# Attention's normalisation moved to a compact reciprocal by way of DRAM, and the SSD decay difference moved to a bias

## The chip, the cores and the metric

The kernel runs on one NeuronCore of a Trainium2 chip. The engines are named as in the profile: PE (TensorE, with its weight loads PEld), DVE (VectorE), ACT (ScalarE), POOL (GpSimd), and SP (SyncE), which issues all DMAs. Times are device microseconds of one launch. Of the kernel before there are three timed runs.

## The reference

Two layers of a hybrid block over 1024 tokens and 256 context tokens, width 1024, in fp32. Each layer makes all branches with one projection, runs an SSD scan in both directions, attention with 12 query heads on 4 key heads, and a convolution branch, and projects the joined result back.

```python
def attend(q, keys, vals):                      # per block of queries
    s = jnp.einsum('bqkrd,bskd->bkrqs', qi, keys) * scale
    p = jax.nn.softmax(s, axis=-1)
    return jnp.einsum('bkrqs,bskd->bqkrd', p, vals)
...
attn_lat = attend(ql, [kl, kc], [vl, vc]) * jax.nn.silu(ga)     # 1024 queries, 1280 keys
attn_ctx = attend(qc, kc, vc) * jax.nn.silu(ga_c)               # first layer only: 256 queries, 256 keys
...
# SSD, in chunks of 128 tokens
cum  = jnp.cumsum(dt * A, axis=2)
seg  = cum[:, :, :, None] - cum[:, :, None, :]
lmat = jnp.exp(jnp.where(mask, seg, -jnp.inf))
y_diag = jnp.einsum('bclsg,bclsgr,bcsgrp->bclgrp', cb, lmat, xdt)
```

The change touches the division in the softmax, which is made after the product with the values, and `seg`.

## The kernel before

Each layer has four stages: the norm and the input projection (`phase_b`), in which the convolutions run on VectorE beside the matmuls; attention (`attn`) together with the SSD scan (`ssd`); and the output projection (`out_half`) in two halves of 512 columns. Intermediate tensors go through DRAM (`q_d`, `k_d`, `ga_d`, `ya_d`, `cum_d` and others).

The instructions are not in program order. Each piece of code sets a due time with `at(us)`, and a scheduler places the instructions of each engine by that time and by its own estimate of when they are ready. The order is fixed at build: an engine, SP's queue too, runs its list in order, and an instruction that waits holds all behind it.

Attention is cut into units: a pair of heads `p` (six) and a block `g` of 256 queries. The first layer has five blocks a pair, four of latent tokens with ten key tiles and one of context tokens with two; the second layer has four. That makes 30 + 24 = 54 units. Four generators interleave. `maxima` takes the row maxima of unit i+2: score matmuls `q_a` by `k_a` into PSUM tiles `m` (four banks), emptied by VectorE into `a_sm`. `scores` makes the scores of unit i again, transposed, ScalarE puts their exponentials into `a_p`, and VectorE or GpSimd add the tiles up in `a_ac`; `a_a2` (in the profile `a_a`) is the sum of the two halves of that. `values` multiplies `a_p` by the values `vs` into half of a PSUM tile `t` (two buffers) and loads the gate `a_g`. `finish`, one unit later, sums `a_a` over the keys with a matmul by a matrix of twos into the other half of `t`. That gives twice the denominator, which the 64 partitions of a head all hold, since `ga_d` holds twice the silu. VectorE inverts it (`a_rc`), multiplies, GpSimd multiplies by the gate, and SP stores to `ya_d`.

In `ssd`, per chunk, four blocks of six heads are loaded from `cum_d` spread over the partitions (`s_cb`, two buffers); GpSimd subtracts the cumulative sum of the partition's own token, ScalarE takes Relu and Exp in place (`s_e`), and GpSimd multiplies by the masked product `s_cm`. PE uses `s_e` in the matmuls `x<-s_e,s_xd`. Ten chunks with output in the first layer, eight in the second. All matmuls of `q_a`, `k_a` and the weights are in fp32r; `a_p` by `vs`, `a_a` by `twos` and `s_e` by `s_xd` are fp32, and each of those stands as two instructions in the trace.

Of the kernel before, what the change touches and what calls it, by code (L numbers as in the profile page):

```python
# [10 lines left out]
AF = mybir.ActivationFunctionType  # L11
ALU = mybir.AluOpType
# [14 lines left out]
AHEAD = 2  # L27
FLAG = 7
NG = [0, 1]
A2B = 1  # L30
GATP = True
GB = 2
XLAG = 34
PVB = (4, 6)
DM = 1024
# [125 lines left out]
def build(tc, a, out, depth=DEPTH, dump=None):  # L161
    nc = tc.nc
    es = ExitStack()
    V, S, G, P, Y = nc.vector, nc.scalar, nc.gpsimd, nc.tensor, nc.sync
# [9 lines left out]
    def mk(p, shape, tag, dt=F32, bufs=None):  # L174
        uid[0] += 1
        k = {} if bufs is None else {"bufs": bufs}
        return p.tile(shape, dt, tag=tag, name=f"{tag}_{uid[0]}", **k)
# [8 lines left out]
    def dr(shape, name, dt=F32):  # L186
        t = dp.tile(shape, dt, tag=name, name=name)
        if dump is not None:
            dump[name] = t
        return t  # L190

    def mm(o, l, r, start, stop):
        P.matmul(o, l, r, start=start, stop=stop)  # L193
# [4 lines left out]
    def act(o, i, f, **k):  # L198
        S.activation(o, i, f, **k)  # L199
# [28 lines left out]
    twos = mk(cp, [128, 64], "twos")  # L228
# [35 lines left out]
    ys_d = dr([6, 128, T], "ys_d")  # L264
    ya_d = dr([6, 128, T], "ya_d")
    yc_d = dr([4, 128, T], "yc_d")
    gt_d = [dr([2, DM], f"gt_d{l}") for l in range(depth)]

    def rs_pow(o, i, scale, tmp, n):
# [440 lines left out]
    def ssd(l, sp, c0, sv):  # L710
# [3 lines left out]
        dt, cum, ec, et, wd = sv  # L714
# [11 lines left out]
        def bc(x, n=NH, w=HD):  # L726
            return x.unsqueeze(2).to_broadcast([128, n, w])
# [27 lines left out]
        for c in [8, 9] + list(range(8)):  # L755
# [3 lines left out]
            if c < 8 or not last:  # L759
# [7 lines left out]
                ps = mk(px, [128, 512], "x")  # L767
# [12 lines left out]
                for g in range(2):  # L780
                    for d in range(2):
                        h0 = 12 * d + 6 * g
                        cb = mk(sp, [128, 6, 128], "s_cb", bufs=2)
                        src = cum_d[24 * c + h0:24 * c + h0 + 6, :].rearrange("h t -> (h t)")
                        Y.dma_start(out=cb.rearrange("p h t -> p (h t)"),
                                    in_=src.unsqueeze(0).to_broadcast([128, 768]))
                        e = mk(sp, [128, 6, 128], "s_e", bufs=4)
                        G.tensor_tensor(e, cb, bc(cum[:, c, h0:h0 + 6], 6, 128), ALU.subtract)
                        act(e, e, AF.Relu, scale=-1.0)
                        act(e, e, AF.Exp, scale=-1.0)  # L790
                        G.tensor_tensor(e, e, cm[:, d, g].unsqueeze(1).to_broadcast([128, 6, 128]), ALU.mult)
                        E[d, g] = e
                yo = mk(sp, [128, 768], "s_yo", bufs=1)
                G.tensor_tensor(hv(yo), hv(xt), bc(rc(l, "d")), ALU.mult)
                for d, hin in enumerate((hf, hb[c])):
# [3 lines left out]
                    for g in range(2):  # L799
                        ps = mk(px, [128, 512], "x")  # L800
                        mm(ps[:, 0:384], cT[:, g, :], hin[:, 384 * g:384 * g + 384], True, True)
                        h0 = 12 * d + 6 * g
# [5 lines left out]
                for g in range(2):  # L808
                    ps = mk(px, [128, 512], "x")
                    for f3 in range(3):  # L810
                        f = 3 * g + f3
# [17 lines left out]
                ps = mk(px, [128, 512], "x")  # L829
# [74 lines left out]
    def attn(l, ap, c0, pre):  # L904
# [3 lines left out]
        def key_tiles(i):  # L908
            return range(NT) if units[i][1] < 4 else range(8, NT)

        def kv(i, x):
            return (2 * units[i][0] + x) // 3
# [31 lines left out]
        pts, acs = {}, {}  # L944


        def scores(i):
            qa, qb = qst.pop(i)
            pts[i] = {}
            kt = key_tiles(i)  # L950
            ng = NG[i % len(NG)] if len(kt) > 2 else 0
            ac = [mk(ap, [128, 2, 512], f"a_ac{x}") for x in range(2)] if len(kt) > 2 else None
            prev = []
            same = kv(i, 0) == kv(i, 1)
            for b in kt:
                ps = mk(pm, [128, 512], "m")
                for x in range(1 if same else 2):
                    ka, kb = kst[kv(i, x)]
                    o = ps if same else ps[:, 256 * x:256 * x + 256]
                    ra = qa.rearrange("p x t q -> p (x t q)") if same else qa[:, x].rearrange("p t q -> p (t q)")  # L960
                    rb = qb.rearrange("p x t q -> p (x t q)") if same else qb[:, x].rearrange("p t q -> p (t q)")
                    mm(o, ka[:, b, :], ra, True, False)
                    mm(o, kb[:, b, :], rb, False, True)
                if b % 2 == 0:
                    pt2 = mk(ap, [128, 2, 512], "a_p", bufs=PTB)
                act(pt2[:, b % 2], ps, AF.Exp)
                pts[i][b] = pt2[:, b % 2]
                if b % 2:
                    j = b // 2
                    if not prev or j == ng + 1:  # L970
                        prev.append(pt2)
                    else:
                        e, o = (G, ac[0]) if j <= ng else (V, ac[1])
                        e.tensor_tensor(o, prev[-1], pt2, ALU.add)  # L974
                        prev[-1] = o
                yield
            if len(prev) > 1:
                V.tensor_tensor(ac[1], prev[0], prev[1], ALU.add)  # L978
                prev = [ac[1]]
            a2 = mk(ap, [128, 512], "a_a2", bufs=A2B)  # L980
            V.tensor_tensor(a2, prev[0][:, 0], prev[0][:, 1], ALU.add)
            acs[i] = a2
            yield

        def values(i):
            p, g = units[i]
            kt = key_tiles(i)
            gat = mk(ap, [128, 256], "a_g", bufs=GB)
            Y.dma_start(out=gat, in_=ga_d[p][:, 256 * g:256 * g + 256])
# [13 lines left out]
        def finish(i, ps, gat):  # L1003
            p, g = units[i]
            a2 = acs.pop(i)
            for y in range(2):
                mm(ps[64 * y:64 * y + 64, 1, :], twos[:, 0:64], a2[:, 256 * y:256 * y + 256], True, True)
            rc_ = mk(ap, [128, 256], "a_rc", bufs=1)
            V.reciprocal(rc_, ps[:, 1])  # L1009
            V.tensor_tensor(rc_, ps[:, 0], rc_, ALU.mult)  # L1010
            (G if GATP else V).tensor_tensor(gat, gat, rc_, ALU.mult)
            Y.dma_start(out=ya_d[p][:, 256 * g:256 * g + 256], in_=gat)

        t0 = c0
# [18 lines left out]
        for i in range(nu):  # L1033
            at(t0)
            prep(i + AHEAD + 1, t0 - 4)
            w = (13.2 if units[i][1] < 4 else 3.4) * AT_PACE
            ga = maxima(i + AHEAD) if i + AHEAD < nu else ()
            gb = scores(i)
            vq.append(values(i))
            nb = len(key_tiles(i))  # L1040
            na = 0 if i + AHEAD >= nu else 13 if units[i + AHEAD][1] < 4 else 5
            ia = 0
            for s in range(nb):
                at(t0 + w * s / nb)
                next(gb)
                while ia < na and ia * (nb - 1) <= s * na:
                    next(ga)
                    ia += 1
                step += 1
                if step > VLAG:  # L1050
                    pump()
                if fin and s == FLAG % nb:
                    finish(*fin.pop(0))
            for _ in gb:
                pass
            for _ in ga:
                pass
            t0 += w
        while vq:
            pump()  # L1060
        while fin:
            finish(*fin.pop(0))
# [58 lines left out]
    def layer(l, nh, b0):  # L1121
# [8 lines left out]
        ap = pool(st, f"ap{l}")  # L1130
        sp = sr.enter_context(tc.tile_pool(name=f"sp{l}", bufs=1, side="right"))
        ssd(l, sp, c0, sv)
        sr.close()
        yp = sr.enter_context(tc.tile_pool(name=f"yp{l}", bufs=1, side="right"))
# [72 lines left out]
```

## Time and profile before

| what | value |
|---|---|
| three runs | 2912.45, 2925.26, 2928.9 us |
| median | 2925.26 us |
| the profiled execution's own time | 2925.86 us |
| its span | 2924.0 us |
| mean granted TensorE clock | 0.976 |
| first attention stage, from the span's start | 826 to 1385 us |
| second attention stage | 2240 to 2745 us |

The page's first part gives the busy time of each engine, the second part the same in 40 equal slices (a digit is tenths of the slice; PEclk is the granted clock). In a row of groups the columns are line, engine, operation, output and input tile, shape and count, then busy time in us and mean ns of one, then the idle time before them and who ended it. A matmul's length overlaps with its neighbours'. In a row of waits the three numbers are the total us, the times, and the longest. In a row of windows each engine's busy time stands with its count of instructions; behind them the granted clock, the DMA share and GB/s.

### The profile page before, as it was taken

To read this page: it belongs to the slowest core of one execution; us is meant where nothing else is said; L and a number is where in the kernel's file an instruction comes from. 1 tells how busy PE (TensorE), PEld (TensorE's weight loads), DVE (VectorE), ACT (ScalarE), POOL (GpSimd) and SP (SyncE) were. 2 spreads that over 40 slices of the span, in tenths; PEclk is the share of its full clock that TensorE was granted. 3 is DMA by queue.
4 is the path that set the end of the run, shared out by engine and by line. 5 is a ranking of instruction groups with operands and counts; after the bars stand their busy time and mean duration, and the time that the engine had idled before them with its cause. 6 is when DMAs were issued, how large, how long until landed. Compare 5 with 4: busy or idle time off the path is not lost. (4 is left out here: it accounts for less than half of the span.)

```text
span 2924.0 us, 41060 instructions
## 1 busy us (share of the span) xinstructions
PE 2775.7 (95%) x15708; PEld 2058.5 (70%) x15708; DVE 2167.2 (74%) x2987; ACT 1068.0 (37%) x1801; POOL 1167.3 (40%) x832
## 2 busy tenths in 40 slices
PE   5999998999999999899999999999998999999998
PEld 3888876888855555565787998877886565555676
DVE  4576899973288889887545577999834889898744
ACT  4212221222245555454335322222223455644532
POOL 2244122232166767662112353122322676775111
PEclk8999998999999999999999999999999999999999
DMA  6541111223342323223745322113335232321654
GB/s 237 191 160 66 56 55 62 92 92 112 101 144 84 102 68 104 67 76 99 213 153 161 122 77 68 56 55 98 111 118 168 74 98 77 95 64 43 185 154 144
DMA packets 284035, 314.44 MB, mean 108 GB/s; under 512 B 27606, under 2 KB 219190, under 8 KB 282814
## 3 DMA queue, kind: packets, MB, share of 16 engines
q1 hardware_dynamic: 283838, 311.82, 33.5%
q8 instruction: 123, 2.02, 0.3%
q14 instruction: 74, 0.61, 0.1%
HBM read 236.25 MB, written 75.50 MB: 107 GB/s over the span
## 5 line engine op out<-in xcount | busy, mean ns | idle before, releaser
L193 PE MATMUL m<-hh,wth 128*128 128x512 f32 (+1 forms) x1440 | 534.9, 371 | 0.1
L193 PE MATMUL m<-hl,wth 128*128 128x512 f32 (+1 forms) x1440 | 533.4, 370 | 0.0
L193 PE MATMUL m<-hh,wtl 128*128 128x512 f32 (+1 forms) x1440 | 532.7, 370 | 0.0
L199 ACT ACTIVATE a_p<-m 128x512 f32<-128x512 f32 x492 | 289.0, 595 | 374.0 <-PE m L193 370.6
L208 DVE SCALAR_TENSOR_TENSOR cac<-up,cmw,cac 128x1295 f32<-128x1295 f32 (+1 forms) x240 | 385.4, 1627 | 2.0
L935 DVE TENSOR_REDUCE a_sm<-m 128x1 f32<-128x512 f32 (+1 forms) x600 | 332.5, 582 | 46.9 <-PE m L193 45.0
L359 POOL TENSOR_TENSOR wtl<-wr,wth 128x1024 fp32r<-128x1024 f32 x68 | 200.3, 2945 | 406.6 <-ACT wth L199 406.6
L193 PE MATMUL t<-a_p,vs 128*64 128x256 f32 x1968 | 324.0, 405 | 0.7 <-DVE a_rc L1010 0.3
L193 PEld LDWEIGHTS m<-hh,wth 128*128 128x128 f32 x1440 | 274.0, 190 | 48.0 <-ACT th L199 0.5
L193 PEld LDWEIGHTS m<-hh,wtl 128*128 128x128 f32 x1440 | 273.5, 190 | 48.3
L193 PEld LDWEIGHTS m<-hl,wth 128*128 128x128 f32 x1440 | 273.8, 190 | 47.4
L193 PE MATMUL m<-q_a,k_a 128*128 128x512 f32 (+1 forms) x656 | 259.7, 406 | 6.1 <-DVE a_sm L935 4.6
L193 PE MATMUL m<-k_a,q_a 128*128 128x512 f32 (+1 forms) x600 | 247.0, 437 | 13.6 <-DVE a_sm L935 9.8
L193 PE MATMUL m<-woh,yh 128*128 128x512 f32 x576 | 225.8, 395 | 8.2 <-issue 3.3
L193 PE MATMUL m<-woh,yl 128*128 128x512 f32 x576 | 228.8, 398 | 4.4 <-DVE yl L1099 4.3
L193 PE MATMUL m<-wol,yh 128*128 128x512 f32 x576 | 226.5, 394 | 0.0
L193 PE MATMUL m<-q_b,k_b 65*128 65x512 f32 (+1 forms) x656 | 218.8, 344 | 0.0
L193 PEld LDWEIGHTS m<-q_a,k_a 128*128 128x128 f32 x656 | 125.9, 192 | 107.1 <-issue 52.0
L193 PEld LDWEIGHTS t<-a_p,vs 128*64 128x64 f32 x1968 | 104.3, 136 | 133.9 <-issue 95.3
L193 PEld LDWEIGHTS m<-k_a,q_a 128*128 128x128 f32 x600 | 113.5, 195 | 113.3 <-issue 45.2
L199 ACT ACTIVATE wth<-wr 128x1024 fp32r<-128x1024 f32 (+1 forms) x84 | 89.3, 1064 | 256.3 <-DMA wr<-in_wfm 134.5
L193 PE MATMUL m<-wth,hh 128*128 128x256 f32 (+1 forms) x608 | 173.7, 288 | 0.6 <-DVE c_qn L474 0.5
(239 smaller groups left out, 5604.4 us busy)
## 6 DMA issues: line engine op xcount, KB each, us to landing
wr<-in_wfm SPq DMA_DIRECT2D x68, 512.0 KB, 3.6
s_cb<-cum_d SPq DMA_DIRECT2D x72, 384.0 KB, 3.7
ada_w<-in_adaw SPq DMA_DIRECT2D x32, 512.0 KB, 4.2
wor<-in_wout SPq DMA_DIRECT2D x64, 256.0 KB, 3.1
s_x<-xt_d SPq DMA_DIRECT2D x38, 384.0 KB, 3.0
yf<-ys_d SPq DMA_DIRECT2D x36, 384.0 KB, 4.0
yf<-ya_d SPq DMA_DIRECT2D x36, 384.0 KB, 4.2
yf<-yc_d SPq DMA_DIRECT2D x36, 256.0 KB, 2.9
```

The costliest lines, as they stand in the source:

```text
L193: P.matmul(o, l, r, start=start, stop=stop)
L199: S.activation(o, i, f, **k)
L208: V.scalar_tensor_tensor(o, i, s, i1, op0, op1)
L359: (e or G).tensor_tensor(lo[:, s], raw, hi[:, s].bitcast(F32), ALU.subtract)
L935: V.tensor_reduce(sm[:, 2 * x + t, j:j + 1], ps[:, 0:kn], axis=AX.X, op=ALU.max)
```

## The change

In `finish`, the two halves of the last sum are no longer added on VectorE: PE multiplies both by `twos` and adds them in PSUM. ScalarE copies the whole of `t` (the product with the values and the denominators) to SBUF, `a_un`, with a single buffer. One row of denominators per head is stored to DRAM (`dn_d`), loaded again as 32 partitions of 16 (`a_r`), inverted there by VectorE, stored to `rn_d`, and loaded spread over 64 partitions per head (`a_rb`). GpSimd multiplies the gate first by the copy, then by the inverse. The gate tile gets a third buffer. The sum of a context unit is now its tile `a_p` itself, and that of a full unit `a_ac`, which keeps its single buffer.

In `ssd`, the subtraction on GpSimd is gone. ScalarE takes Relu directly from `s_cb`, head by head, with the cumulative sum as bias: six instructions of 128 columns where one of 768 stood.

```diff
-A2B = 1
-GATP = True
-GB = 2
+GB = 3
...
+    dn_d = [dr([2, 256], f"dn_d{i}") for i in range(30)]
+    rn_d = [dr([2, 256], f"rn_d{i}") for i in range(30)]
...
                         e = mk(sp, [128, 6, 128], "s_e", bufs=4)
-                        G.tensor_tensor(e, cb, bc(cum[:, c, h0:h0 + 6], 6, 128), ALU.subtract)
-                        act(e, e, AF.Relu, scale=-1.0)
+                        for j in range(6):
+                            act(e[:, j], cb[:, j], AF.Relu, scale=-1.0, bias=cum[:, c, h0 + j:h0 + j + 1])
                         act(e, e, AF.Exp, scale=-1.0)
...
-            a2 = mk(ap, [128, 512], "a_a2", bufs=A2B)
-            V.tensor_tensor(a2, prev[0][:, 0], prev[0][:, 1], ALU.add)
-            acs[i] = a2
+            acs[i] = prev[0]
...
             a2 = acs.pop(i)
+            for k in range(2):
+                for y in range(2):
+                    mm(ps[64 * y:64 * y + 64, 1, :], twos[:, 0:64], a2[:, k, 256 * y:256 * y + 256], k == 0, k == 1)
+            un = mk(ap, [128, 2, 256], "a_un", bufs=1)
+            act(un, ps, AF.Copy)
             for y in range(2):
-                mm(ps[64 * y:64 * y + 64, 1, :], twos[:, 0:64], a2[:, 256 * y:256 * y + 256], True, True)
-            rc_ = mk(ap, [128, 256], "a_rc", bufs=1)
-            V.reciprocal(rc_, ps[:, 1])
-            V.tensor_tensor(rc_, ps[:, 0], rc_, ALU.mult)
-            (G if GATP else V).tensor_tensor(gat, gat, rc_, ALU.mult)
+                Y.dma_start(out=dn_d[i][y:y + 1, :], in_=un[64 * y:64 * y + 1, 1, :])
+            G.tensor_tensor(gat, gat, un[:, 0], ALU.mult)
+            r = mk(ap, [32, 16], "a_r", bufs=2)
+            Y.dma_start(out=r, in_=dn_d[i].rearrange("y (a q) -> (y a) q", q=16))
+            V.reciprocal(r, r)
+            Y.dma_start(out=rn_d[i].rearrange("y (a q) -> (y a) q", q=16), in_=r)
+            rb = mk(ap, [128, 256], "a_rb", bufs=1)
+            for y in range(2):
+                Y.dma_start(out=rb[64 * y:64 * y + 64], in_=rn_d[i][y:y + 1, :].to_broadcast([64, 256]))
+            G.tensor_tensor(gat, gat, rb, ALU.mult)
             Y.dma_start(out=ya_d[p][:, 256 * g:256 * g + 256], in_=gat)
```

The scheduler makes a new order for the two attention stages from this; ahead of the first one, TensorE's order is the same. Three places follow, in the order of the built programs. A count behind a row is equal instructions in a row, and an fp32 matmul counts once here.

TensorE in the second layer, where the ones-matmul of a unit stands between the scores and values of the next. Before:

```order
L193 MATMUL m_22126<-q_a_21588,k_a_20937 128x512
L193 MATMUL m_22126<-q_b_21589,k_b_20938 128x512
L193 MATMUL t_21932<-a_a_4309_22062,twos_80 64x256 x2
L193 MATMUL t_22092<-a_p_22103,vs_19305 64x256 x2
L193 MATMUL m_22131<-k_a_20937,q_a_21912 128x256
L193 MATMUL m_22134<-q_a_21588,k_a_20937 128x512
```

After, one such place:

```order
L194 MATMUL v_22235<-idr_76,q_g_22232 128x128 x4
L191 MATMUL t_22089<-a_ac_4184_22074,twos_80 64x256 x4
L191 MATMUL m_22287<-k_a_19797,q_a_22069 128x512
L191 MATMUL t_22260<-a_p_22275,vs_19795 64x256
L191 MATMUL m_22290<-k_a_19797,q_a_22069 128x512
```

Four matmuls by `twos` stand where two stood, and read `a_ac` itself.

ScalarE in the first layer, where the fifth pair's context unit (`a_p_11100` before, `a_p_12235` after) follows its last full unit and the sixth pair begins. Before:

```order
L199 ACTIVATE a_p_11100<-m_11110 128x512
L199 ACTIVATE s_e_7873<-s_e_7873 128x768 x2
L199 ACTIVATE q_a_11093<-v_11088 128x512
L199 ACTIVATE q_b_11094<-v_11088 64x512
L199 ACTIVATE q_g_11331<-q_t_11329 128x4x64
L199 ACTIVATE s_of_7820<-s_yz_7779 128x768
L199 ACTIVATE s_e_7880<-s_e_7880 128x768 x2
L199 ACTIVATE s_e_7887<-s_e_7887 128x768 x2
L199 ACTIVATE a_p_11188<-m_11183 128x512
```

After:

```order
L197 ACTIVATE a_p_12235<-m_12245 128x512
L197 ACTIVATE q_a_12226<-v_12221 128x512
L197 ACTIVATE q_b_12227<-v_12221 64x512
L197 ACTIVATE q_g_12466<-q_t_12464 128x4x64
L197 ACTIVATE a_un_12299<-t_12075 128x512
L197 ACTIVATE a_un_12417<-t_12244 128x512
L197 ACTIVATE a_p_12332<-m_12329 128x512
L197 ACTIVATE a_p_12332<-m_12342 128x512
```

The copies of the full unit and of the context unit stand one behind the other, in one buffer, ahead of the next unit's first exponential. The same pair stands at each of the first five context units.

SP's queue in the second layer. Before, the store of a unit's result and the loads around it:

```order
L785 DMA s_cb_19985<-cum_d 128x768
L785 DMA s_cb_19992<-cum_d 128x768
L873 DMA q_t_22543<-q_d_125 128x2x128
L828 DMA ys_d<-s_yo_19814 128x6x128
L1012 DMA ya_d<-a_g_21768 128x256
L989 DMA a_g_22090<-ga_d_137 128x256
L720 DMA s_b_19967<-bt_d 128x256
```

After:

```order
L1010 DMA dn_d_155<-a_un_22847 1x256 x2
L764 DMA s_cT_20655<-cT_d 128x2x128
L1013 DMA a_r_22852<-dn_d_155 32x16
L1015 DMA rn_d_185<-a_r_22852 32x16
L1018 DMA a_rb_22856<-rn_d_185 64x256 x2
L785 DMA s_cb_20545<-cum_d 128x768
L1020 DMA ya_d<-a_g_22600 128x256
L785 DMA s_cb_20556<-cum_d 128x768
L987 DMA a_g_23124<-ga_d_137 128x256
```

The six transfers of a unit's denominators stand in the queue, each but the first waiting for the one before it to land, and the decay loads `s_cb` stand behind them.

## The prediction

> **What bounds the kernel now.** I read the page's busy line and its slices first, to see which engine is full and where.
>
> ```profile
> PE 2775.7 (95%) x15708; PEld 2058.5 (70%) x15708; DVE 2167.2 (74%) x2987; ACT 1068.0 (37%) x1801; POOL 1167.3 (40%) x832
> ...
> PE   5999998999999999899999999999998999999998
> ...
> DVE  4576899973288889887545577999834889898744
> ```
>
> TensorE is full nearly throughout. The change lies in the two attention stages (slices 12 to 19 and 31 to 38), so the view of windows comes next, cut to them.
>
> ```profile
> core 0: us, PE busy (x) PEld busy (x) DVE busy (x) ACT busy (x) POOL busy (x), PEclk, DMA share, GB/s
> 826.00:1385.00 559.00, 531.35 (x3313) 312.57 (x3314) 479.57 (x673) 284.73 (x483) 352.03 (x212) 0.97 0.28 85
> 2240.00:2745.00 505.00, 494.10 (x3032) 286.82 (x3031) 449.10 (x634) 262.80 (x449) 322.01 (x188) 0.99 0.29 90
> ```
>
> Of 1064 us TensorE is idle for 27.65 + 10.90 = 38.55. VectorE is busy 87%, ScalarE 51%, GpSimd 63%. So a gain can only come out of TensorE's idle time and its lowered clock (0.97 and 0.99), and each matmul added is paid almost whole. The waits of TensorE say who makes it idle:
>
> ```profile
> PE m L193 <- DVE a_sm L935: 14.4, 18, 2.2
> ...
> PE t L193 <- DVE a_a L981: 13.0, 9, 3.6
> ```
>
> Both are VectorE: the row maxima that empty score banks (`a_sm`), and the halves' sum (`a_a`) that the ones-matmul waits for. One boundary after a short context unit, in the timeline, shows how the second arises:
>
> ```profile
> 917.33 1.74 DVE L1009 RECIPROCAL a_rc<-t 128x256 f32<-128x256 f32 x1
> ...
> 918.99 0.91 DVE L981 TENSOR_TENSOR a_a<-a_p 128x512 f32<-128x512 f32 x1
> ...
> 919.96 1.12 PE L193 MATMUL t<-a_a,twos 128*64 128x256 f32 x4 [2.13 <-DVE a_a L981]
> ```
>
> The reciprocal of the last full unit stands in front of the sum, and TensorE stops for 2.13 us. Behind such stops the granted clock halves for 7 us:
>
> ```profile
> 919.00:926.00 7.00, 6.04 (x25) 4.74 (x26) 5.78 (x13) 1.51 (x3) 3.12 (x4) 0.51 0.21 74
> 1011.00:1018.00 7.00, 6.74 (x18) 2.85 (x17) 5.39 (x10) 1.79 (x3) 4.58 (x4) 0.52 0.28 94
> 1175.00:1182.00 7.00, 6.31 (x19) 4.13 (x19) 4.44 (x6) 2.81 (x6) 5.48 (x4) 0.51 0.12 37
> 1209.00:1216.00 7.00, 6.45 (x20) 4.38 (x20) 7.00 (x16) 1.38 (x3) 3.51 (x5) 0.52 0.43 133
> ```
>
> **TensorE: halves summed in PSUM.** Each of 54 units gets two more 256-column matmuls with `twos`, four more instructions in the trace. Rows of the timeline, start and length:
>
> ```profile
> 1366.33 1.08 PE L193 MATMUL t<-a_p,vs 128*64 128x256 f32 x8
> ...
> 2426.69 0.65 PE L193 MATMUL t<-a_a,twos 128*64 128x256 f32 x4 [0.39 <-DVE a_a L981]
> ```
>
> Eight in a row take 1.08 us and four take 0.65, of the same shape: 0.43 for four more, x54 = **+23.2 us**. Nothing hides it. Ends: +12 if half falls into stops that stay, +35 (54 x 0.65) if the new ones never join the old.
>
> **VectorE: what leaves.**
>
> ```profile
> L981 DVE TENSOR_TENSOR a_a<-a_ac 128x512 f32<-128x512 f32 x48 | 57.8, 1205 | 0.2
> L1009 DVE RECIPROCAL a_rc<-t 128x256 f32<-128x256 f32 x54 | 94.5, 1750 | 2.4 <-PE t L193 2.0
> L1010 DVE TENSOR_TENSOR a_rc<-t,a_rc 128x256 f32<-128x256 f32 x54 | 22.3, 412 | 0.1
> ```
>
> Those are 174.6 us. What comes instead, a reciprocal over 16 columns, I estimate at 0.16 us by scaling 1750 ns down by columns and adding some 50 ns: 9 us in all. VectorE falls from 87% to about 72%. Worth to the end: the 13.0 us of waits on `a_a` go, since no such sum is left, and I take two thirds of the 14.4 on `a_sm`, because the additions `a_ac` of 1.2 to 2.8 us still stand among the maxima: **-22.6 us**. Ends: -13 (only `a_a`) and -38.6 (all idle time). Of the clock, the four windows above cost 4 x 7 x 0.485 = 13.6 us. Two of them stand at the boundaries where `a_a` was late, so I take half: **-6.8 us**, ends 0 and -13.6.
>
> **GpSimd: one subtraction less, one product more.**
>
> ```profile
> L788 POOL TENSOR_TENSOR s_e<-s_cb,d_cum 128x768 f32<-128x768 f32 x72 | 117.8, 1646 | 55.0 <-PE x L193 51.6 <-DMA s_cb<-cum_d 3.3
> L1011 POOL TENSOR_TENSOR a_g<-a_g,a_rc 128x256 f32<-128x256 f32 x54 | 52.6, 974 | 104.2 <-DVE a_rc L1010 98.6 <-DVE s_rs L205 5.5
> ```
>
> -117.8 and +52.6: GpSimd does 65 us less, and what makes TensorE wait, above, is VectorE, so 0. Its second product waits for the inverse from DRAM; queued behind it are the masked decays, for which TensorE waits last of all in a chunk, while attention's matmuls go on; that covers it. If it does not, TensorE stops at the chunk's products with decays, and the price is of the size of rival (3).
>
> **ScalarE: six biased Relus for one, and a copy.** The nearest rows are a run of four 128x128 activations with a scale and a bias operand, and the same 1024 columns with and without one such operand; beside them, three of the 768-column kind in a row, and the exponentials of the scores.
>
> ```profile
> 48.72 1.49 ACT L199 ACTIVATE n_h<-x,msh,msc 128x128 f32<-128x128 f32 x4
> ...
> L199 ACT ACTIVATE n_h<-x,msh,msc 128x128 f32<-128x128 f32 x80 | 30.0, 458 | 8.6 <-PE x L196 7.5 <-POOL hl L346 0.9 <-DVE msc L208 0.2
> ...
> L199 ACT ACTIVATE n_x<-n_x,n_ss 128x1024 f32<-128x1024 f32 x20 | 22.8, 1149 | 9.9 <-POOL n_ss L271 9.9
> L199 ACT ACTIVATE hl<-n_x 128x1024 fp32r<-128x1024 f32 x20 | 21.2, 1060 | 50.6 <-DMA n_x<-x_d 35.1 <-DMA n_x<-in_xin 15.4
> ...
> 2648.12 2.44 ACT L199 ACTIVATE s_e<-s_e 128x768 f32<-128x768 f32 x3
> ...
> L199 ACT ACTIVATE a_p<-m 128x512 f32<-128x512 f32 x492 | 289.0, 595 | 374.0 <-PE m L193 370.6
> ```
>
> Four cost 1.49, so they follow each other every (1.49 - 0.458)/3 = 0.344 us; less one operand (1149 - 1060 = 89 ns) that is 0.255. Six are 1.53 us, in place of (2.44 - 0.84)/2 = 0.80: +0.73, x72 = 53 us. The copy of 128x512 out of PSUM has the shape of the exponentials `a_p`, 0.595 us, x54 = 32 us. Over the stage ScalarE goes to 59%, which hides it. It does not where a chunk's decays are made. Two such stretches:
>
> ```profile
> 1045.40:1059.80 14.40, 14.40 (x101) 8.36 (x99) 11.61 (x16) 11.56 (x18) 12.96 (x8) 1.00 0.55 170
> 2493.90:2508.00 14.10, 13.94 (x97) 7.91 (x96) 11.34 (x14) 12.57 (x18) 12.81 (x8) 1.00 0.55 170
> ```
>
> ScalarE is busy 12.07 of 14.25 us there; 4 x 0.73 and mostly one copy make 15.5, so some 1.2 us too much in each. TensorE waits for exponentials only if nothing else is ready, so I take a third, over 18 chunks: **+7 us**. Ends: 0, and at 0.344 per Relu (5.65 added, 3.5 too much, x18) +63.
>
> The Trainium skill (ScalarE: Activation LUTs, What ACT_TABLE_LOAD costs) gives an activation with one pointer operand 280 ns and 0.833 ns a column, and lets neighbours overlap by 93 ns. By that, as an estimate, a Relu of 128 columns costs 0.294 us, six 1.76, and this term +13 instead of +7: 2939 in all. Its 93 ns per operand agrees with the 89 here.
>
> **The chain through DRAM.** Per unit SyncE gets six more entries, and four landings in sequence. Rows of DMA issues, the last number the landing:
>
> ```profile
> a_g<-ga_d SPq DMA_DIRECT2D x54, 128.0 KB, 2.2
> ya_d<-a_g SPq DMA_DIRECT2D x54, 128.0 KB, 1.9
> s_cb<-cum_d SPq DMA_DIRECT2D x72, 384.0 KB, 3.7
> ```
>
> About 8 us per unit of some 20, in which SyncE's later loads wait. Nothing needs the product before the output projection. I charge 0; ends 0 and the rival's. One place cannot hide: `a_un` has a single buffer, and at the five boundaries full unit, context unit, next unit, ScalarE's order has both copies back to back. The second waits until the two rows of the first have landed: about 0.4 + 2.0 = 2.4 us, with the next unit's exponentials queued behind it. VectorE's short reciprocals wait there too, ahead of maxima. Half of it reaches TensorE: **+6 us**; ends 0 and 5 x 2.4, or 5 x (2.4 + 3.4) = 29 where the clock halves.
>
> **Sum.** +23.2 - 22.6 - 6.8 + 7 + 6 = +6.8 us. The profiled execution took 2925.86 us (span 2924.0), beside a median of 2925.26, so **2933 us**: no change. About 0.5%, 14.6 us, is what can be told from none.
>
> **Rivals.** (1) *Faster, VectorE was worth more.* Every idle microsecond of TensorE and the four clock windows hang on VectorE's queue, and the new waits stay hidden: 23.2 - 38.6 - 13.6 = -29, 2897 us. For it: 52 us more of waits lie before weight loads, mostly covered, that the view of waits puts to `a_sm`; and VectorE's additions vary widely:
>
> ```profile
> PEld m L193 <- DVE a_sm L935: 52.1, 104, 2.4
> ...
> L974 DVE TENSOR_TENSOR a_ac<-a_ac,a_p x72: 1160/1346/2802, 839.4 to 2730.9; 128x1024 f32<-128x1024 f32 x72
> ```
>
> If the slow ones are those beside GpSimd's work, 65 us less of it shortens them. The Trainium skill (GPSIMD Engine Reference, Specifications) says the two share SBUF interfaces when VectorE reads two SBUF inputs, which would do just that. Against it: waits for keys, queries and exponentials share that idle time. 25%.
>
> (2) *Slower, ScalarE bounds the decay stretches.* At 0.344 per Relu the term is 63 for 7: 2989 us. It decides from 15 us on, that is once 0.8 us a chunk reach TensorE. For it: ScalarE is busy 85% of those stretches already, and its order is fixed. Against it: outside them it idles half the time, and TensorE can take maxima first. 10%.
>
> (3) *Slower, SyncE.* A decay load held behind a chain makes ScalarE, which now reads `s_cb` itself, wait with exponentials behind it; half of the landing of 3.7 us, x18 = +33: 2966 us. Against it: two `s_cb` buffers let the next chunk's first loads go out early. It decides once a chunk loses 0.5 us. 8%.
>
> (4) *Slower, the single `a_un`.* The five stops halve the clock: 29 for 6, 2956 us. For it: the stops of this length that the trace has now did that. Against it: they fall where maxima of two units are ready, work that needs no exponential. 12%.
>
> The forecast keeps 45%, its own range 2918 to 2950. Below 2911.3 lies most of (1); above 2940.5 lie (2) to (4) and a quarter of the forecast: faster 0.20, same 0.39, slower 0.41. With a tenth left out at each end the range is 2897 to 2972.
>
> **What the profile after would show.** `twos` doubled, and about 0.43 us more where it stands; no wait of TensorE on `a_a`; VectorE near 72% in the two stages; waits on `a_sm` down to a third. A Relu every 0.25 to 0.30 us. ScalarE idle before the second `a_un` of a pair until a DMA lands. Wrong would be: TensorE waiting for `a_p` by tens of microseconds, the slow `a_ac` gone, or more half-clock windows than now.

## The result, and the profile after

The changed kernel took 3007.15 us in the median of four runs (2994.18 to 3010.66), beside 2926.87 for the kernel before: a ratio of 1.0277 with an interval of 1.0232 to 1.0322, or 80 us slower. The forecast was 2933 us, and the range ended at 2972. The profiled execution took 3010.66 us, its span 3008.9.

The busy line of the page after, and three rows of its slices:

```profile
PE 2837.8 (94%) x15924; PEld 2088.7 (69%) x15924; DVE 1992.8 (66%) x2879; ACT 1161.4 (39%) x2215; POOL 1079.6 (36%) x814
...
PE   6999998999899989899999999989998999999998
...
DVE  4476999953376656666445577999735766767444
...
PEclk8999998999998989999999999999999999999999
```

VectorE fell from 74 to 66% of the span (in the two attention stages, by the windows below, from 87 to 67%, where 72 was forecast), and yet TensorE's row has more eights there. The view of windows, cut from the first exponential of the scores to the last product with values, shows how much. First before, then after:

```profile
826.00:1371.00 545.00, 520.61 (x3271) 304.98 (x3272) 468.49 (x660) 280.73 (x477) 351.29 (x212) 0.97 0.27 82
2254.00:2734.00 480.00, 471.11 (x2945) 271.76 (x2945) 427.00 (x596) 250.44 (x430) 309.03 (x179) 0.99 0.27 82
```

```profile
824.00:1416.00 592.00, 556.68 (x3396) 322.45 (x3397) 388.94 (x615) 333.89 (x695) 305.03 (x203) 0.94 0.29 88
2300.00:2819.00 519.00, 498.30 (x3038) 285.92 (x3038) 360.64 (x558) 291.87 (x598) 275.89 (x172) 0.96 0.28 84
```

The stages grew from 1025 to 1111 us, by 86, which is the whole loss; the profiled spans lie 84.9 apart. Three things make it up. TensorE's idle time (length less PE busy) rose from 33.3 to 56.0: +23. Time lost to the clock, which I reckon as the length times (1 less the granted clock) and which is good to some 5 us because the view rounds, rose from 21 to 56: +35. And the matmuls by `twos`, 36.1 us before (a row of groups, x216), are 58.4 + 7.2:

```profile
L191 PE MATMUL t<-a_ac,twos 128*64 128x256 f32 x384 | 58.4, 418 | 7.8 <-DVE a_ac L978 7.7
...
L191 PE MATMUL t<-a_p,twos 128*64 128x256 f32 x48 | 7.2, 388 | 0.0
```

That is +29.5, of which the slower clock is part. The rows of waits say who makes TensorE idle now:

```profile
PE m L191 <- DVE a_sm L935: 19.2, 26, 1.9
PE t L191 <- DVE a_ac L978: 7.7, 7, 2.3
...
PE m L191 <- ACT a_p L197: 7.1, 7, 1.7
PE x L191 <- DVE s_s L825: 6.8, 6, 2.2
...
PE t L191 <- ACT a_p L197: 4.3, 4, 2.3
```

The last three of them read, in the kernel before:

```profile
PE x L193 <- DVE s_s L825: 1.3, 2, 0.9
PE m L193 <- ACT a_p L199: 1.1, 4, 0.4
...
PE t L193 <- ACT a_p L199: 0.3, 1, 0.3
```

The waits on `a_a` are gone, and `a_ac` has taken part of their place. Those on `a_sm` have not fallen (14.4 before), though VectorE does 146 us less in the stages. Three rows have grown: the two of exponentials `a_p`, and that of `s_s`, the sum of squares that the matmul `x<-ones,s_s` reads. ScalarE stands ahead of both. Its groups show the biased Relus, and what it waited for before them:

```profile
L197 ACT ACTIVATE s_e<-s_cb,d_cum 128x128 f32<-128x128 f32 x432 | 132.6, 390 | 46.2 <-PE x L191 29.2 <-DMA s_cb<-cum_d 7.7 <-DVE a_sm L935 5.5
```

One place in the second layer, from the timeline (start, length, what ended the idle time before it), shows the whole path:

```profile
2442.60 0.61 PE L191 MATMUL x<-s_e,s_xd 128*64 128x128 f32 x8
2443.08 3.62 ACT L197 ACTIVATE s_e<-s_cb,d_cum 128x128 f32<-128x128 f32 x12 [1.36 <-PE x L191]
...
2446.61 0.57 ACT L197 ACTIVATE a_p<-m 128x512 f32<-128x512 f32 x1
...
2447.49 0.56 DVE L820 TENSOR_TENSOR s_yz<-x,s_gz 128x384 f32<-128x384 f32 x1 [1.95 <-PE x L191]
...
2450.58 1.86 ACT L197 ACTIVATE s_e<-s_cb,d_cum 128x128 f32<-128x128 f32 x6 [1.92 <-DMA s_cb<-cum_d]
...
2452.34 0.57 ACT L197 ACTIVATE a_p<-m 128x512 f32<-128x512 f32 x1
...
2452.82 0.83 ACT L197 ACTIVATE s_of<-s_yz 128x768 f32<-128x768 f32 x1
...
2452.97 0.84 PE L191 MATMUL t<-a_p,vs 128*64 128x256 f32 x4 [2.35 <-ACT a_p L197]
```

A product of TensorE with the old decays frees `s_e`. ScalarE has stood waiting for that (1.36 us), and runs twelve Relus in a row for 3.62 us; the exponential queued behind them starts at 2446.61. Later six more wait 1.92 us for their load, and an exponential and the chunk's square (`s_of`) stand behind: the square starts 4.8 us after its input was there, and TensorE stops for 2.35 us. The windows ahead of that point and behind it:

```profile
2443.00:2453.00 10.00, 7.65 (x79) 5.87 (x75) 4.24 (x9) 8.00 (x23) 5.06 (x4) 1.00 0.46 152
```

```profile
2453.50:2460.50 7.00, 7.00 (x30) 4.37 (x28) 4.58 (x7) 6.93 (x17) 2.18 (x3) 0.50 0.63 181
```

TensorE was busy 7.65 of 10 us, and the clock is halved for the next 7. The Trainium skill (TensorE: Matmul & The Clock Gate, Why this matters for your kernels) warns of idle gaps over about 3 us. Here a single stop of 2.35 sufficed. Another place of the same profile has only two stops in the 10 us ahead of it, of 0.55 and 0.52 us, and there the clock halves for longer:

```profile
941.40:951.40 10.00, 8.94 (x84) 6.62 (x83) 5.18 (x10) 10.00 (x30) 4.95 (x4) 1.00 0.42 132
951.50:965.00 13.50, 12.59 (x43) 6.51 (x41) 7.48 (x12) 6.20 (x11) 3.14 (x3) 0.50 0.46 147
```

What decides whether a stop is followed by a halved clock these runs don't show.

In the kernel before, a boundary of chunks (this one in the first layer) reads:

```profile
1047.73 0.61 PE L193 MATMUL x<-s_e,s_xd 128*64 128x128 f32 x8
...
1048.39 0.56 DVE L820 TENSOR_TENSOR s_yz<-x,s_gz 128x384 f32<-128x384 f32 x1 [2.32 <-PE x L193]
...
1049.16 0.60 ACT L199 ACTIVATE a_p<-m 128x512 f32<-128x512 f32 x1
1049.64 1.47 POOL L788 TENSOR_TENSOR s_e<-s_cb,d_cum 128x768 f32<-128x768 f32 x1
1049.65 0.84 ACT L199 ACTIVATE s_of<-s_yz 128x768 f32<-128x768 f32 x1
```

There GpSimd takes up the freed `s_e`, after work of its own, and the exponential and the square are through before its subtraction ends and a Relu can start. At the same boundary in e1 (below), which has the bias part of the change alone, ScalarE waits and then runs twelve Relus, and two exponentials come behind them:

```profile
1050.76 3.62 ACT L199 ACTIVATE s_e<-s_cb,d_cum 128x128 f32<-128x128 f32 x12 [1.91 <-PE x L193]
...
1054.29 1.06 ACT L199 ACTIVATE a_p<-m 128x512 f32<-128x512 f32 x2
```

### The profile page after: what moved, and what is told of

Same layout as the page of the kernel before. It is cut to its first block, busy times and chain, and to the rows that moved or that the text cites. A ratio compares the mean times of both kernels' runs of the same rounds, so it can differ in the third digit from the quotient of the medians.

```text
span 3008.9 us, 42378 instructions
## 1 busy us (share of the span) xinstructions
PE 2837.8 (94%) x15924; PEld 2088.7 (69%) x15924; DVE 1992.8 (66%) x2879; ACT 1161.4 (39%) x2215; POOL 1079.6 (36%) x814
## 5 line engine op out<-in xcount | busy, mean ns | idle before, releaser
L935 DVE TENSOR_REDUCE a_sm<-m 128x1 f32<-128x512 f32 (+1 forms) x600 | 338.9, 586 | 145.8 <-PE m L191 143.2
L191 PE MATMUL t<-a_p,vs 128*64 128x256 f32 x1968 | 336.0, 419 | 4.3 <-ACT a_p L197 4.3
```

Source lines behind the costliest of these rows:

```text
L935: V.tensor_reduce(sm[:, 2 * x + t, j:j + 1], ps[:, 0:kn], axis=AX.X, op=ALU.max)
```

## The experiments

All times are medians; each ratio is to the kernel before on the same chip. "Lost to the clock" and "idle" are reckoned as above from each kernel's own two windows. "Squares late" is, for each of the 18 chunks, the time from the end of its later product `s_yz` to the start of its square, added up from the timeline (a dash where ScalarE makes no square). The last four columns are those of the profiled execution, which in e2 and e6 took 8 us more than the median.

| kernel | us | to before | ACT busy in the stages | TensorE idle | lost to the clock | squares late |
|---|---|---|---|---|---|---|
| before | 2926.87 | | 531 | 33 | 21 | 6.9 |
| after | 3007.15 | +80.3 | 626 | 56 | 56 | 60.5 |
| e1 bias alone | 2984.56 | +54.8 | 596 | 56 | 60 | 49.9 |
| e2 denominators alone | 2935.85 | +6.0 | 560 | 28 | 11 | 15.3 |
| e4 Relu cut, no bias | 2935.33 | +5.5 | 563 | 41 | 32 | 15.3 |
| e5 Relu cut, bias of zeros | 2948.52 | +19.9 | 599 | 50 | 32 | 24.3 |
| e6 bias, due times spread | 2965.77 | +37.2 | 596 | 54 | 50 | 51.5 |
| e9 bias, square on GpSimd | 2967.08 | +40.5 | 578 | 52 | 32 | - |
| e11 after, Relus paced | 2944.83 | +15.2 | 620 | 36 | 15 | 33.7 |
| e12 after, square on GpSimd | 2978.64 | +49.0 | 610 | 44 | 27 | - |

**Which part.** The theories were: A, ScalarE, whose Relus hold up exponentials; B, the chain of the denominators; C, that any change moves this order to a worse one. Four kernels told them apart. Each is the kernel before with:

```diff
 e1   - GpSimd's subtraction, one Relu          + six biased Relus (the change's own)
 e2   + all of the change but the bias part
 e3   + halves summed by twos; reciprocal and both products stay as before
 e4   - act(e, e, AF.Relu, scale=-1.0)
      + for j in range(6): act(e[:, j], e[:, j], AF.Relu, scale=-1.0)     # the subtraction stays
```

> The kernel before with the bias part alone: six biased Relus of 128 columns straight from s_cb, no subtraction on GpSimd; denominators as before. Theory A (ScalarE in the decay stretches: exponentials come late behind the Relus, TensorE stops and its clock halves) expects the larger part of the 80 us: +40 to +65 us. Theory B (the denominators' chain with its new waits carries the loss) expects within 10 us of the kernel before. Theory C (any change of the code makes the scheduler lay out a worse order, whatever it is) expects a loss of 20 us or more here and in every other variant as well.

2984.56 us, 1.0184 (1.0155 to 1.0213). A holds in size; B can't make this, since the denominators are untouched.

> The changed kernel with the old decay difference put back (subtraction on GpSimd, one Relu of 768 columns): halves on TensorE, copy, DRAM chain and two products stay. Theory A expects +10 to +35 us over the kernel before (23 us of matmuls, less VectorE's waits, plus the copy). Theory B expects +60 to +80 us. Theory C expects +20 us or more.

2935.85 us, 1.0028 (1.0014 to 1.0042). B falls.

> The kernel before with the halves summed on TensorE alone (four matmuls by twos, no sum of halves on VectorE; reciprocal over 256 columns, product and gate as before). The prediction's terms give +23 us for the matmuls, -13 us for the waits on the sum of halves and some -7 us of clock: 0 to +10 us. If the matmuls are paid whole and the relief of VectorE is worth nothing: +23 us. Theory C expects +20 us or more.

2938.55 us, 1.0023 (1.0007 to 1.0038). So the reciprocal's way through DRAM, with the copy, the transfers and 104 us less on VectorE (12.8 us of short reciprocals in e2, for 94.6 + 22.3), adds nothing that can be told to the halves.

> The kernel before with the Relu of 768 columns cut into six of 128 without bias; the subtraction stays on GpSimd. This loads ScalarE alone, with about 0.2 us for each Relu by the trace (0.292 us between biased ones, less some 0.09 for the operand): 6 x 0.2 - 0.73 = +0.47 us, x72 = 34 us of ScalarE, against 73 us in the bias variant. Theory A expects a loss of about half that of the bias variant, +15 to +30 us. If the loss of the bias variant comes from something else in it (the wait for the decay load moved to ScalarE, GpSimd's order), this one is within 10 us of the kernel before.

2935.33 us, 1.0019 (1.0004 to 1.0034). C falls: four new orders of the same kernel, and three of them cost 9 us or less. But A's 15 to 30 us are missed too. These Relus follow each other every 0.20 us, so ScalarE bore about half of the added time, and a tenth of the loss. The parts e1 and e2 add up to 61, while the change lost 80.

**Time or order.** Theory T says that ScalarE's time costs, O that it is when the Relus come.

```diff
 e5   before, with  act(e[:, j], e[:, j], AF.Relu, scale=-1.0, bias=zc[:, 0:1])   # zc = 0; the subtraction stays
 e6   e1, with  at(t0 - SSD_PACE + 5 * (2 * g + d))  ahead of each of a chunk's four blocks
```

> The kernel before, with its subtraction on GpSimd kept and its Relu of 768 columns cut into six of 128 that each read a bias (a column of zeros): what is computed stays the same. ScalarE then issues the same biased Relus as in the bias part alone (0.292 us apart, six 1.75 for 0.84, about +65 us over 72 blocks), but each block's Relus still come one subtraction (1.65 us of GpSimd) after another, and GpSimd keeps its 118 us. Theory T (ScalarE's time alone costs): as the bias part alone, 2965 to 2990. Theory O (it is the order: with the subtraction gone, the Relus of a chunk's blocks need only a load, are ready together, and are laid in a row ahead of the scores' exponentials): near the unbiased cut (2935), 2930 to 2945, with at most some 15 stretches of decay work over 3 us on ScalarE (13 in the unbiased cut, 28 in the bias part alone).

2948.52 us, 1.0072 (1.0051 to 1.0094): between the two ranges, with 15 of O's long stretches. The windows of e1, then of e5:

```profile
825.00:1397.00 572.00, 539.38 (x3280) 314.12 (x3282) 467.85 (x662) 314.86 (x659) 291.28 (x176) 0.94 0.27 81
2276.00:2799.00 523.00, 499.27 (x2952) 285.97 (x2953) 429.35 (x606) 280.69 (x577) 255.10 (x150) 0.95 0.26 79
```

```profile
824.00:1387.00 563.00, 535.12 (x3298) 311.27 (x3296) 469.25 (x671) 317.52 (x665) 355.87 (x212) 0.96 0.28 84
2261.00:2759.00 498.00, 475.74 (x2943) 274.60 (x2943) 436.84 (x605) 281.16 (x579) 303.58 (x178) 0.98 0.27 82
```

ScalarE is busy for the same 596 and 599 us, GpSimd 113 us longer in e5, and e5 is 35 us faster. The other 20 us go with ScalarE's 68 us more of time, the subtraction being in place; so both theories own a part, and O the larger. In the changed kernel the same Relus cost less (e11, below).

> The kernel before with the bias part alone, and the four decay blocks of a chunk given due times 5 us apart instead of one due time for all four. ScalarE's time is that of the bias part alone (2984.56). Theory T (ScalarE's time): 2970 to 2990, no change from it. Theory O (the order): more than half of the 54 us comes back, 2957 or less, and the half-clock time of the two attention stages falls from 123 us to below 75.

2965.77 us, 1.0138 (1.0115 to 1.0162). 18 of 55 us came back, less than O's "more than half" and more than T allows. The time lost to the clock fell from 60 us to 50, where O's 75 us of half clock would make it 38, and the squares are as late as in e1. New due times alone don't pace the Relus.

**The square.** Theory N: the loss comes by way of the late square; E: by way of the exponentials.

```diff
 e9 (on e1), e12 (on the change)
-                act(sq, yz, AF.Square)
+                G.tensor_tensor(sq, yz, yz, ALU.mult)
```

> The kernel before with the bias part alone, and the square of a chunk's output (`s_of`, 768 columns, one for each of 18 chunks) taken from ScalarE to GpSimd, which has lost 118 us of subtraction. ScalarE keeps the biased Relus and loses 18 x 0.84 = 15 us. In the bias part alone this square began 49.9 us in all after its input was there (6.9 before), and TensorE stood behind it at the ones-matmul `x<-ones,s_s`. Theory N (the loss comes by way of the late square): more than half of the 54 us returns, 2957 or less, waits of TensorE on `s_s` near 2 us. Theory E (it comes by way of the scores' exponentials, 82 us late behind decay work): 2970 to 2985, half-clock time in the stages still over 90 us. Both in part: 2957 to 2970.

2967.08 us, 1.0147 (1.0123 to 1.0171). By the differences to before 14 us came back, a quarter: both in part.

> The changed kernel with the square of a chunk's output taken from ScalarE to GpSimd, as was done with the bias part alone, where 17.5 us came back. If the late square (60.5 us in all here) does the same harm in the changed kernel: 2980 to 2993. If the extra 18 us of the changed kernel come by way of the square as well: 2962 to 2980. If it doesn't matter here: 3000 to 3012.

2978.64 us, 1.0177 (1.0149 to 1.0205): 31 of 80 us came back, twice as much as in e9. With the square off ScalarE over a third of the change's loss is gone, some of the extra 19 us included. ScalarE also has 16 us less to do (610 for 626), and this run doesn't tell the late square from that.

**The change with its Relus paced.** The changed kernel, with the subtraction on GpSimd and e5's six Relus with a bias of zeros behind it:

> The changed kernel with the subtraction put back on GpSimd, and the six Relus per block kept as biased ones (a column of zeros as bias): ScalarE has the changed kernel's whole time, copies and biased Relus, but each block's Relus come behind a subtraction of 1.65 us. Alone the denominators cost +8 and the biased Relus behind a subtraction +20; together they and the bias part without subtraction cost +80, which is 18 more than the parts. Theory P (the pacing: without the subtraction a chunk's Relus start at once when TensorE frees `s_e`, ahead of exponentials and of the square): 2950 to 2962, the sum of the two parts, square late by less than 35 us in all (60.5 in the changed kernel). Theory L (the load: copies and Relus together are what ScalarE can't hold): 2975 to 3000, square late by more than 45 us.

2944.83 us, 1.0055 (1.0030 to 1.0079). Below P's 2950, and far from L's 2975. Its windows, beside those of after above:

```profile
825.00:1372.00 547.00, 527.25 (x3396) 312.97 (x3396) 397.79 (x612) 329.61 (x692) 372.01 (x239) 0.99 0.31 93
2255.00:2754.00 499.00, 482.99 (x3034) 281.25 (x3032) 375.15 (x557) 290.75 (x599) 316.12 (x201) 0.98 0.30 88
```

ScalarE is as busy as in the changed kernel, 620 for 626 us, GpSimd 107 us busier; 65 us are gone, 41 of them of the clock and 20 of idle time. The wait for TensorE to free `s_e` stands on GpSimd again, and ScalarE's idle time before its Relus is 20.1 us for 46.2:

```profile
L790 POOL TENSOR_TENSOR s_e<-s_cb,d_cum 128x768 f32<-128x768 f32 x72 | 116.3, 1626 | 53.0 <-PE x L191 45.7 <-DMA s_cb<-cum_d 7.4
L197 ACT ACTIVATE s_e<-s_e,zc 128x128 f32<-128x128 f32 x432 | 133.7, 393 | 20.1 <-POOL s_e L790 19.7
```

So the load on ScalarE was bearable, and the removed subtraction is what cost. As every run here, e11 has an order of its own, and the 65 us hold that too; the new orders of e2, e3 and e4 cost 9 us or less, their work included. No run takes the subtraction away without cutting the Relu, since the bias is another for each head.

**Relus off ScalarE, two misses.**

```diff
 e7 (on e2)      - act(e, e, AF.Relu, scale=-1.0)    + ts(V, e, e, 0.0, ALU.min)   # then Exp without the sign
 e10 (on before) - subtraction, Relu   + for j in range(6): ts(G, e[:, j], cb[:, j], cum[...h0 + j], ALU.subtract, 0.0, ALU.min)
```

> The changed kernel without its bias part (subtraction on GpSimd), and the Relu taken off ScalarE: VectorE takes the minimum with 0 over 768 columns, about 0.73 us by the 0.50 of 512 columns, and the exponential follows without a sign. ScalarE loses 72 x 0.80 = 58 us, VectorE gains 53. If ScalarE's time in the decay stretches is a bound already at the level before (theory T): 5 to 20 us below the denominators alone (2935.85), that is 2915 to 2931, faster than both kernels at its lower end. If VectorE is the tighter of the two there: 2937 to 2960, with waits for row maxima above 14 us again. If neither: 2931 to 2937.

2983.39 us, 1.0195 (1.0171 to 1.0219): over all three expectations. The groups of e7:

```profile
L201 DVE TENSOR_SCALAR s_e<-s_e 128x768 f32<-128x768 f32 x72 | 85.0, 1184 | 9.3 <-POOL s_e L788 9.3
...
L197 ACT ACTIVATE s_e<-s_e 128x768 f32<-128x768 f32 x72 | 60.0, 842 | 87.5 <-DVE s_e L201 86.7 <-DMA s_cT<-cT_d 0.5
```

The minimum took 1.18 us and not 0.73, but worse, ScalarE now stands waiting for it, 86.7 us in all, in a list that holds the scores' exponentials too.

> The kernel before with the opposite of the bias part: GpSimd subtracts and takes the minimum with 0 in one instruction per head (six of 128 columns in place of one subtraction of 768), and ScalarE has no Relu at all: 58 us less of it in the attention stages. If a GpSimd instruction of 128 columns takes about 0.35 us, GpSimd has 33 us more. If ScalarE's decay work costs time already in the kernel before (the exponentials there start 82 us late in all): 2905 to 2922. If it costs nothing at that level: 2924 to 2935. If GpSimd becomes the bound of the decay stretches (a 128-column instruction of 0.6 us or more, 14 us for the four blocks of a chunk): 2940 to 2990, with TensorE waiting for `s_e`.

3168.9 us, 1.0825 (1.0797 to 1.0852), past the worst case. The group of GpSimd, and TensorE's first wait:

```profile
L205 POOL TENSOR_SCALAR s_e<-s_cb,d_cum 128x128 f32<-128x128 f32 x432 | 342.1, 809 | 46.1 <-PE x L193 28.1 <-issue 7.2 <-DMA s_cb<-cum_d 6.2
```

```profile
PE x L193 <- DVE s_of L803: 82.6, 12, 22.5
```

Six of them are 4.9 us for 1.65. TensorE doesn't wait for `s_e` in that row, as the third case had it, but for VectorE, and the timeline shows a place where VectorE stands still beside GpSimd:

```profile
1063.35 12.02 DVE L981 TENSOR_TENSOR a_a<-a_ac 128x512 f32<-128x512 f32 x1
...
1067.74 7.08 POOL L791 TENSOR_TENSOR s_e<-s_e,s_cm 128x768 f32<-128x768 f32 x4
...
1075.43 1.12 PE L193 MATMUL t<-a_a,twos 128*64 128x256 f32 x4 [7.38 <-DVE a_a L981]
```

A sum of 0.69 us (the median of its kind) took 12.02. GpSimd ran without a break from 1059.28 to 1074.82, and the sum ended 0.55 us later. Eleven of VectorE's sums `a_ac` and `a_a` in e10 took over 4 us; the longest in the kernel before took 2.80. So a busier GpSimd reached TensorE by way of VectorE; how much of the 242 us went that way isn't shown.

**What of the pacing does the harm.** Open was whether it is ScalarE's wait for `s_e`, or the burst behind it. Both kernels write the Relus in place:

```diff
 e13 (on the change), e14 (on e1)
-  act(e[:, j], cb[:, j], AF.Relu, ...);  act(e, e, AF.Exp, scale=-1.0)
+  act(cb[:, j], cb[:, j], AF.Relu, ...); act(e, cb, AF.Exp, scale=-1.0)
```

> The changed kernel with the biased Relus written in place, into `s_cb`; the decays' exponential reads `s_cb` and writes `s_e`. The first two blocks' Relus of a chunk (two `s_cb` buffers) then need only their load and can run before TensorE frees `s_e`, so the work that starts when it does is 2 x 0.84 us instead of 3.6; `s_cb` is held until the exponential has read it, and the next load comes later. If the burst after the release does the harm: 2960 to 2990, square late by less than 45 us in all (60.5 in the changed kernel). If it is the wait on ScalarE itself, which now stands at the exponential: 2995 to 3015. If the later loads of `s_cb` take its place: over 3015, ScalarE waiting for `s_cb` by over 30 us (7.7 in the changed kernel).

3015.87 us, 1.0294 (1.0263 to 1.0324), on the border of the second and the third case; the 50.0 us of waits for `s_cb` are the third's sign. ScalarE's groups in e13:

```profile
L197 ACT ACTIVATE s_cb<-s_cb,d_cum 128x128 f32<-128x128 f32 x432 | 133.2, 391 | 56.9 <-DMA s_cb<-cum_d 50.0 <-DVE a_sm L935 5.7 <-DMA s_x<-xt_d 1.0
L197 ACT ACTIVATE s_e<-s_cb 128x768 f32<-128x768 f32 x72 | 58.7, 836 | 26.4 <-PE x L191 26.2
```

> The kernel before with the bias part alone (2984.56), its Relus in place in `s_cb` as in the run before this. If the burst after the release does the harm: 2945 to 2972. If it is the wait on ScalarE: 2977 to 2992. If the later loads take its place: over 2992.

2976.75 us, 1.0170 (1.0139 to 1.0200), at the edge of the second case and inside e1's interval. In e13 ScalarE now waits for the loads (50.0 us, 7.7 in the change) and still for TensorE (26.2 for 29.2). Its stretches of decay work over 3 us with nothing else between fell from 32 in the change to 19, but those over 4 us are ten for nine, and the squares are later still (69.6 us for 60.5). So one wait took the other's place, and which side of the pacing does the harm stays open.

**A version that beats both.** The kernel before, with halves summed by `twos` for the six context units alone:

```diff
 scores:  if len(kt) == 2: acs[i] = prev[0]      # else the sum a_a2 on VectorE, as before
 finish:  for k in range(2): mm(..., twos[:, 0:64], a2[:, k, ...], k == 0, k == 1)   # where units[i][1] == 4
```

> The kernel before with the halves' sum of the context units alone on TensorE (12 of 54 units at most; the full units keep their sum on VectorE). It pays about 0.43 us of twos for each context unit (6 of them, 2.6 us) and takes away the wait for the sum behind the last full unit's reciprocal, the 2.13 us stop and its half clock. If the prediction's reading of the boundary is right: 2910 to 2924, some 5 to 15 us faster than before. Rival (the wait moves to the reciprocal itself or to the row maxima behind it): 2924 to 2935, no change.

2922.94 us, 0.9973 (0.9956 to 0.9990): 6 us faster. TensorE's wait on `a_a` fell to

```profile
PE t L193 <- DVE a_a L984: 9.4, 7, 3.5
```

from 13.0: a part of the boundary's stops went, at the lower end of what was expected.

## Why the prediction was wrong

The step that failed is the 0 for GpSimd's subtraction, and with it the cover that was taken for ScalarE. The bias part stood in the sum with 0 and +7 us; it costs 55 alone (e1), and 80.3 - 6.0 = 74 in the changed kernel.

- *"VectorE makes TensorE wait, so 0" for GpSimd's subtraction* was the larger fault: 65 us by e11. The prediction quoted GpSimd's row with 51.6 us of idle time before its subtraction, ended by `PE x`, and left it unread: someone has to wait there for TensorE to free `s_e`, and GpSimd could afford it. With the subtraction gone the wait stands on ScalarE (29.2 us), with a burst of Relus behind it, and what is queued behind both are exponentials and squares. Given back to GpSimd, the change costs 15 us instead of 80. Whether the wait or the burst does the harm stays open (e13, e14).
- *The price of a Relu* was 0.255 us; six take 1.86 in the timeline, so they come (1.86 - 0.39)/5 = 0.294 apart. That is 0.2 us a block and the smaller fault: for the +7, the same Relus behind a subtraction cost 20 us in e5, and 15.2 - 6.0 = 9 in e11. The Trainium skill (ScalarE: Activation LUTs, What ACT_TABLE_LOAD costs), as quoted there, gave the 0.294.
- *"Only if nothing else is ready", a third.* TensorE's list is fixed too, and holds `x<-ones,s_s` behind the square; that consumer was not in the prediction at all.
- *The clock* was to give 6.8 us, by the windows behind `a_a`. The four windows in the prediction are 13.6 of the 21 us that the stages lost. With the denominators alone the clock gave about 10 (21 to 11 in the table); in the change it took 35. Stops made elsewhere halve it as well.
- *VectorE, -22.6*: near only in its own rows, and where ScalarE is left alone. In e2 the waits on `a_sm` fell from 14.4 to 6.6, those on `a_a` (13.0) went, and 3.4 on `a_ac` came: 17.4 less. Other waits grew, and TensorE's idle time as a whole fell by 6 us (33 to 28). In the change the two rows are 19.2 and 7.7.
- *`twos`, +23.2*: 23.6 by the rows of e2 (52.7 + 7.0 for 36.1), and 29.5 in the change, with the slower clock in it.
- *`a_un`, +6, and the chain, 0*: ScalarE waited 4.3 us for `dn_d`, TensorE not at all in a row of its own; GpSimd stood 166.5 us waiting for `a_rb`, hidden as said. All terms but the Relus' came to -0.2 us; e2 measured +6.0 (4 to 12 by its interval). That is near by luck in part: idle time gave less than forecast, and the clock more.

The rival that came nearest was (2), 2989 us at 10%, and for a wrong reason: it priced a Relu of 0.344 us, where 0.294 came, and not the order. Its argument against, that ScalarE idles half the time outside those stretches, was a share of busy time where the question was what stands first in the list. Rival (3) had ScalarE waiting for `s_cb` with exponentials behind it: 7.7 us of that came, in the place shown above too, but e1, which has no chain through DRAM, loses 55 us as well. Of the prediction's signs of being wrong, more half-clock time came; waits for `a_p` by tens of microseconds did not (11.4 in all).

## What to carry to other kernels

Before an operation is taken off an engine with slack, look at what ended the idle time before it: here that wait didn't go with the operation, it moved to the next engine in the chain, with a burst of work behind it, and exponentials and squares behind both in that engine's fixed list came late. Price a moved step by its place in the list, and by who consumes the work behind it, not by the receiving engine's busy share. Then add the clock: on a TensorE that is 95% busy, the added stops cost 23 us here and the halved clock behind them 35.

## What the runs showed of the hardware

- An operand for the bias costs a ScalarE activation of 128 columns 0.09 us: 0.20 apart without (six in 1.31 us in e4's timeline, 0.30 the last), 0.294 with.
- The TensorE clock halved behind a single stop of 2.35 us, and behind two of 0.55 and 0.52 us.
- A VectorE sum of two halves in SBUF, 128x512, took 12.02 us beside an unbroken run of GpSimd instructions in e10, and 0.69 at the median.
- GpSimd's two-operation instruction with a per-partition scalar took 0.809 us for 128 columns, while its subtraction of 768 columns took 1.65.
- VectorE's minimum over 768 columns in SBUF took between 0.54 and 2.47 us (median 1.14), where the forecast scaled 0.50 for 512.
- More work on GpSimd made the kernel faster, twice: by 35 us (e5 against e1) and by 65 (e11 against the change). In e10, with 224 us more, it made it slower by 242.
